# A macaron SwiGLU block on one core: the first products' deferred work in single small pieces, and the next norm's R11 and R22 made behind P2 and P5

## The chip, the core and the metric

The kernel runs on one core of a Trainium2 chip. A core has engines that run their own instruction streams side by side: TensorE (PE, matmuls; PEld is its loading of the stationary operand), VectorE (DVE), ScalarE (ACT), GpSimd (POOL, unused here) and SyncE (SP), which issues the DMA transfers. They meet through semaphores. Each engine runs its instructions in the order in which they stand in its stream. The metric is the device time of one execution in microseconds (us); the kernel before takes 2170.7 us (median of three runs, 2169.77 to 2173.17).

## The reference

One layer on an input x of 1024 tokens x 1024 channels, float32:

```python
def rmsnorm(x, g):
    xf = x.astype(jnp.float32)
    y = xf * lax.rsqrt(jnp.mean(xf * xf, axis=-1, keepdims=True) + NORM_EPS)
    return (y * g.astype(jnp.float32)).astype(x.dtype)

def swiglu_ffn(x, w_in, w_out):
    gate, up = jnp.split(x @ w_in, 2, axis=-1)
    return (jax.nn.silu(gate) * up) @ w_out
...
        h = h + FFN_RES_WEIGHT * swiglu_ffn(rmsnorm(h, norm_ffn1[l]), ffn1_w_in[l], ffn1_w_out[l])
        u = rmsnorm(h, norm_mix[l])
        proj = u @ w_in[l]
...
        h = h + merged @ w_out[l]
        h = h + FFN_RES_WEIGHT * swiglu_ffn(rmsnorm(h, norm_ffn2[l]), ffn2_w_in[l], ffn2_w_out[l])
    return rmsnorm(h, norm_final)
```

The hidden width of a SwiGLU is 2816, so `w_in` is 1024 x 5632. Between the SwiGLUs lie a combined projection, a retention and a pooling branch, their gated merge and an output projection, which the change doesn't touch.

## The kernel before

*Products.* Every large product is done as a 2 x 2 block scheme that trades block products for block sums (seven products of half-size blocks in place of eight). A token-side operand is called R (R11, R12, R21, R22 are its blocks, T1 to T4 and others are their sums and differences); a weight-side combination is S1 to S4 (`a_S`, lines 437, 450 and 454, on DVE). To keep float32 accuracy on the matmul's reduced type, each operand is split in an upper part (ACT, line 158 or 162) and a lower part, the remainder (DVE, line 159 or 163); `mm3` then issues three matmuls, upper x upper (line 178), upper x lower (179), lower x upper (180). A matmul at line 180 thus waits for the lower part of its weights. `mv` is the pool of split token-side operands, 28 tiles; `wS`, `wL`, `ws`, `wx`, `wy` are split weights (combinations, plain blocks and quarter-size sums).

*Stages.* With the times of the profiled execution: the first SwiGLU's input products (names `a_`, to some 410 us); its output products `b` in the order P1 with P6, P2 with P7, P5 (549 to 579 us), P3 (to 609) and P4 (to 639); the projections (`t0`, `t1`, `p0` and so on) with the norm `n2` from 639 us; retention, pooling and merge; the second SwiGLU's input products (`c_`, 1535 to 1945); its output products `d` with the final norm, to the end.

*The input products (`ffn_in`).* A group is one block of 128 gate and 128 up channels in each half of the block scheme; 22 groups are taken in 11 pairs (k and k + 11). When a group's products are evacuated (line 721 and 723 are sums of PSUM banks), `end()` hangs up what remains: the gate is multiplied by the norm's per-token factor (lines 735 and 738), silu is taken on ACT, and up is multiplied by gate (line 741, one instruction of 1024 columns). After the second group of a pair `w1`, `w2` and `w3` form the output products' token-side operands from the two results (lines 752, 753, 757, 762) and store them in R, T, B and T4 in DRAM by DMAs on SP's queue, from which the output products load them. The lines 571 and 582 collect the shared small products in the bank x.

*What sets the order.* A `Flow` runs the steps: each step has a `prep` (loads and splits), called four steps (`LOOK`) ahead, and a `body` (matmuls). Work of no hurry is put into a queue, `flow.add(...)`; after each body `flow.rate` pieces are taken from its head, and `flow.until` takes more where a result is needed at once. After that a scheduler of the tile framework orders the instructions of each engine by priority (the order of the program, with `soon()` ahead) and by its own estimate of what is ready. So a piece taken later is also placed later in DVE's stream, with what is written behind it put ahead. In FFN1's input products the rate is 1 for the first 40 steps and 2 then; in the second SwiGLU it is 1 for 14 steps and 2 then. A pair has 2 x 2 + 3 = 7 pieces.

*Output products and the next norm.* P1 to P7 are accumulated by `onto` and `done` into the sums `bacc`, whose last part is queued. The quarters of the result are final in the order of the products: the block (0,0) after P2, (1,1) after P5, (0,1) after P3 and (1,0) after P4. The next norm `n2` takes its operands from them: `r11`, `r22` (with `p22`, the split), `t1`, `t2`, `t3`, `r21`, `t4_`, four pieces each, and its statistics (`stats`: the sum of squares `n2sum`, the inverse root `n2v`, `n2r`, then its spread over the partitions by the diagonals `n20dg`, `n21dg` and the matmuls `n20b`, `n21b`, and the copies `n2rb`). `end(0)` queues six of these behind P3, `end(1)` the rest behind P4. P5's operands are called `bp5m`, P4's `bp4m`; they come from the same pool `mv` as the norm's.

Of the kernel before, what the change touches and what calls it, by code (L numbers as in the profile page):

```python
# [13 lines left out]
AF = mybir.ActivationFunctionType  # L14
ALU = mybir.AluOpType
ADD, SUB, MUL = ALU.add, ALU.subtract, ALU.mult
# [74 lines left out]
def block_kernel(ctx: ExitStack, tc, x, x_tok, vecs, f1_in, f1_out, w_in, w_v, pool_w, w_ret, w_pool, w_o,  # L91
# [3 lines left out]
    tt = nc.vector.tensor_tensor  # L95
    stt = nc.vector.scalar_tensor_tensor
    act = nc.scalar.activation
# [48 lines left out]
    def half(t, j):  # L146
        return t[:, j * H : (j + 1) * H]
# [553 lines left out]
    def ffn_in(nx, w, ops, name, start=None):  # L701

        R, T, B, T4 = ops
        hid = {}

        def group(g):
            gate_up = {}

            def dest(which):
                tile, j = which  # L710
                if tile not in gate_up:
                    gate_up[tile] = (tl if start and g == 0 else t4)(f"{name}{'gu'[tile]}{g}")
                return half(gate_up[tile], j)

            later = []

            def evac(which, in0, in1):
                tile, j = which
                dst, rms = dest(which), nx.rb
                if in1 is not None:  # L720
                    tt(dst, in0, in1, ADD)
                elif not tile and rms is not None:
                    tt(dst, in0, half(rms, j), MUL)
                    return
                else:
                    copy(dst, in0)
                if not tile:
                    later.append(j)

            def end():  # L730
                gate, up = gate_up[0], gate_up[1]

                def scale():
                    if len(later) == 2:
                        tt(gate, gate, nx.rms(), MUL)
                    else:
                        for j in later:
                            tt(half(gate, j), half(gate, j), half(nx.rms(), j), MUL)
                    act(gate, gate, AF.Silu)

                flow.add(scale, lambda: tt(up, gate, up, MUL))
                hid[g] = up
                k = g % FH
                if g < FH:
                    return
                lo, hi, e = hid.pop(k), up, {}
                R11, R12, R21, R22 = half(lo, 0), half(lo, 1), half(hi, 0), half(hi, 1)

                def w1():

                    e["n"], e["m"] = gate, c2(f"{name}m{k}")
                    tt(half(e["n"], 0), R12, R11, SUB)
                    tt(half(e["n"], 1), R22, R12, SUB)
                    load(B[k], e["n"])

                def w2():
                    tt(R12, R22, half(e["n"], 0), SUB)
                    load(R[k], lo)
                    load(T[k], hi)

                def w3():
                    tt(e["m"], R21, R12, SUB)
                    load(T4[k], e["m"])
                    done.add(k)

                flow.add(w1, w2, w3)

            if start and g == 0:
                return plain_group(nx, start, f"{name}{g}_", evac, end)
            return lambda shared: strassen(nx, w[g, 0], w[g, 1], f"{name}{g}_", evac, end, shared=shared, dest=dest)  # L770

        done = ops_done.setdefault(name, set())
        order = [g for k in range(FH) for g in (k, k + FH)]
        if start:

            return chain(group(0), pairs_of_both(nx, (group(g) for g in order[1:]), BY_OPERAND, 3))
        return pairs_of_both(nx, (group(g) for g in order), BY_OPERAND, 2)
# [31 lines left out]
    def ffn_out(nx, ops, ready, w, res, name, sink, end, last=None):  # L809
# [121 lines left out]
        def done(mt, j, to=sink, scaled=False):  # L931
            q = quarter(mt, j)

            def end():
                if not scaled:
                    scale(q, q, j)
                tt(q, q, old.pop((mt, j)), ADD)
                if to:
                    to(mt, slice(j * H, (j + 1) * H), acc[mt])

            flow.add(end)
# [9 lines left out]
        def after2(i):  # L951
            with soon():
                scale(quarter(i, 0), bk["a", i], 0)
            done(i, 0, scaled=True)

        def after7(i):
            onto(i + 4, 1, "b", i, p1s[i])
# [9 lines left out]
        def after5(i):  # L967
            onto(i + 4, 1, "a", i)
            done(i + 4, 1)

        def after3(i):
            onto(i, 1, "a", i)
            done(i, 1)
            if i == 3:
                end(0)

        def after4(i):
            onto(i + 4, 0, "b", i)
            done(i + 4, 0)
            if i == 3:  # L980
                end(1)

        for k in range(FH):
            yield step("p1", p1, k, "a", True, after1)
# [91 lines left out]

    def ffn1():
        for n, step in enumerate(ffn_in(first, f1_in, ops1, "a", lead)):
            flow.rate = 1 if n < 40 else 2
            yield step  # L1080
        yield from ffn_out(first, ops1, ops_done["a"], f1_out, x, "b", mix.quarter, end1)

    mix = Next("n2", V_MIX, h1)

    def end_of(nx):
        def end(part):
            if part == 0:
                nx.work(nx.r11, nx.r22, nx.t2, nx.t1, nx.t3, nx.p22)
            else:
                nx.work(nx.r21, nx.t4_)  # L1090
                nx.stats()

        return end
# [232 lines left out]
    def projections():  # L1326
        for n, step in enumerate(pairs(mix, (project(*o) for o in order), range(7), 0)):
            if n == 28:
                flow.rate = 1
            yield step  # L1330
        yield from values()
        for o in light[10:]:
            g = project(*o)(())
            yield from (g[m] for m in BY_SUM)
        flow.rate = 2
# [242 lines left out]
    def retention():  # L1578
        filler = fillers()

        def fill(n=1):
            for _ in range(n):
                f = next(filler, None)
                if f is not None:
                    yield f

        yield units[0].operands, units[0].values
        for n, u in enumerate(units):
            after = units[n + 1] if n + 1 < len(units) else None

            def scores(u=u, n=n):
                if u.nh == 1:
                    u.follow(units[n - 1])
                u.scores()

            def rest(u=u, after=after):
                u.products()
                if after:
                    after.operands()
                u.outputs()  # L1600
                if u.nh == 1:
                    u.normalise()

            yield none, scores
            yield none, u.keys
            yield from fill()
            if after:
                yield after.loads, after.values
            yield none, rest

            late = u.nh == 0 and n
            if n < 3 or late:
                yield from fill()
            if late:
                yield none, units[n - 1].finish
        yield none, lambda: take(range(6))
        yield from fill(2)
        yield none, units[-1].finish
        yield none, lambda: take((6, 7))
        yield from fill(2 * KT)  # L1620
# [85 lines left out]
    def merge():  # L1706
        yield from two_by_two(two_groups(0) + two_groups(1), BY_OPERAND, handed(mg, lambda rest: flow.add(*rest)))
        yield from two_by_two((out_group(i) for i in range(4)), BY_OPERAND,
                              handed(ffn2, lambda rest: (flow.add(*rest[:4]), ffn2.stats(between=rest[4:]))))
# [4 lines left out]
    class Last(Norm):  # L1714
# [74 lines left out]
            return r0  # L1789

        def end(self, part):
            tokens = slice(H, S)
            at = {}

            def stats():
                r = inverse_root(token_sums(self.ssq, range(tokens.start // P, tokens.stop // P), "fin0"), D, "fin0")
                at["b"] = spread(r, "fin0")

            def scale(mt):
                t = self.tiles[mt][:, tokens]  # L1800
                stt(t, t, vec[:, V_FINAL + mt : V_FINAL + mt + 1], at["b"], MUL, MUL)
                load(out[mt, :, tokens], t)

            flow.add(stats, *(lambda mt=mt: scale(mt) for mt in range(KT)))
# [2 lines left out]

    def second():
        for n, step in enumerate(ffn_in(ffn2, f2_in, ops2, "c")):
            flow.rate = 1 if n < 14 else 2  # L1810
            yield step
    flow.run(chain(ffn1(), projections(), retention(), merge(), second(),
                   ffn_out(ffn2, ops2, ops_done.setdefault("c", set()), f2_out, h2, "d", fin.quarter, fin.end, fin)))
    flow.some(-1)
# [86 lines left out]
```

## Time and profile before

| | us |
|---|---|
| median of three runs | 2170.7 (2169.77 to 2173.17) |
| profiled execution | 2170.95, span 2169.2 |
| PE busy | 2144.7 (99%) |
| DVE busy | 1839.2 (85%) |
| ACT busy | 1093.4 (50%) |

The span is the time from the first to the last recorded instruction. A row of a timeline gives start and duration in us, the engine, the line of the kernel, the operation, out<-in by the program's names with their numbers left out, the shapes, and in brackets the idle time of the engine before it and what ended it. Matmuls of 512 columns are shown 0.39 us long and start some 0.22 to 0.23 us apart, as they overlap in the array; a start-to-start time above that is a loss. DVE's instructions overlap a little too: one of 512 columns lasts 0.68 us and the next starts 0.60 us after it.

### The profile page before, as it was taken

The numbers are of one execution on the slowest core, as the hardware profiler recorded it, in microseconds if no ns is written. First come the engines' busy times: TensorE is split into PE (matmuls) and PEld (weight loads), VectorE is DVE, ScalarE is ACT, GpSimd is POOL, SyncE is SP. The second block draws the span as 40 slices with busy tenths as digits, with TensorE's granted clock in tenths as the row PEclk, the third lists the DMA queues.
The fourth block names the chain that finished last, engine by engine and source line by source line (L and its number), as shares of the span: only waits on it lengthen the run. The fifth ranks groups of instructions, "written<-read, shape, count | busy, mean of one in ns | idle before, by whom it ended". The sixth has DMA issues, their size and how long they took to land.

```text
span 2169.2 us, 29623 instructions
## 1 busy us (share of the span) xinstructions
PE 2144.7 (99%) x10668; PEld 1811.1 (83%) x10668; DVE 1839.2 (85%) x3180; ACT 1093.4 (50%) x2053; POOL 0.2 (0%) x4
## 2 busy tenths in 40 slices
PE   9999999999998999999999999999999999999998
PEld 7888888888887888888888898887888888888887
DVE  8789788896889798899767877899998878889697
ACT  8544444454646444444426754446644444445454
POOL 0000000000000000000000000000000000000000
PEclk9999999999999999999999999999999999999999
DMA  7233223585533333333485567624132222358633
GB/s 259 85 117 117 91 98 114 168 283 186 174 92 117 117 124 110 107 117 109 155 271 191 165 219 257 222 98 156 68 119 101 107 95 101 117 170 281 194 122 126
DMA packets 120131, 320.91 MB, mean 148 GB/s; under 512 B 13232, under 2 KB 17456, under 8 KB 119984
## 3 DMA queue, kind: packets, MB, share of 16 engines
q1 hardware_dynamic: 119408, 317.98, 43.1%
q8 instruction: 83, 1.36, 0.3%
q10 hardware_dynamic: 576, 1.05, 0.1%
q14 instruction: 64, 0.52, 0.1%
HBM read 228.27 MB, written 90.70 MB: 147 GB/s over the span
## 4 chain that ended last, share of the span: by engine, by line
PE 88%; DVE 8%; DMA 2%; issue 1%; ACT 1%; SPq 0%; ACTq 0%; DVEq 0%
PE c_b L180 2%; PE a_b L180 2%; PE c_b L179 2%; PE a_b L178 2%; PE c_b L178 2%; PE a_b L179 2%; PE a_e L178 1%; PE a_e L180 1%; PE a_e L179 1%; PE bp6b L179 1%; PE bp6b L178 1%; PE bp6b L180 1%; PE a_a L179 1%; PE a_a L178 1%; PE a_a L180 1%
## 5 line engine op out<-in xcount | busy, mean ns | idle before, releaser
L180 PE MATMUL c_b<-n3T,c_wS 128*128 128x512 f32 x176 | 69.3, 394 | 2.4 <-DVE c_wS L159 2.3
L178 PE MATMUL c_b<-n3T,c_wS 128*128 128x512 f32 x176 | 68.3, 390 | 1.4 <-ACT c_wS L158 1.4
L179 PE MATMUL c_b<-n3T,c_wS 128*128 128x512 f32 x176 | 68.5, 389 | 0.0
L180 PE MATMUL a_b<-n1T,a_wS 128*128 128x512 f32 x168 | 65.9, 392 | 2.0 <-DVE a_wS L159 2.0
L178 PE MATMUL a_b<-n1T,a_wS 128*128 128x512 f32 x168 | 65.5, 390 | 1.4 <-ACT a_wS L158 1.4
L179 PE MATMUL a_b<-n1T,a_wS 128*128 128x512 f32 x168 | 65.4, 389 | 0.0
L179 PE MATMUL a_a<-n1R,a_wL 128*128 128x512 f32 x120 | 46.7, 389 | 0.0
L178 PE MATMUL a_a<-n1R,a_wL 128*128 128x512 f32 x120 | 46.7, 389 | 0.0
L180 PE MATMUL a_a<-n1R,a_wL 128*128 128x512 f32 x120 | 46.7, 389 | 0.0
L179 PE MATMUL c_a<-n3R,c_wL 128*128 128x512 f32 x112 | 43.7, 390 | 0.0
L178 PE MATMUL c_a<-n3R,c_wL 128*128 128x512 f32 x112 | 43.6, 389 | 0.0
L180 PE MATMUL c_a<-n3R,c_wL 128*128 128x512 f32 x112 | 43.6, 389 | 0.0
L180 PEld LDWEIGHTS c_b<-n3T,c_wS 128*128 128x128 f32 x176 | 33.0, 188 | 12.1 <-DVE c_wS L159 5.4
L180 PEld LDWEIGHTS a_b<-n1T,a_wS 128*128 128x128 f32 x168 | 31.5, 188 | 10.5 <-DVE a_wS L159 4.1
L178 PEld LDWEIGHTS c_b<-n3T,c_wS 128*128 128x128 f32 x176 | 33.0, 188 | 8.4 <-ACT c_wS L158 1.8
L179 PEld LDWEIGHTS c_b<-n3T,c_wS 128*128 128x128 f32 x176 | 33.0, 188 | 6.9
L178 PEld LDWEIGHTS a_b<-n1T,a_wS 128*128 128x128 f32 x168 | 31.5, 188 | 8.2 <-ACT a_wS L158 1.8
L179 PEld LDWEIGHTS a_b<-n1T,a_wS 128*128 128x128 f32 x168 | 31.5, 188 | 6.5
L158 ACT CAST a_wS<-a_S 128x512 fp32r<-128x512 f32 x45 | 27.1, 621 | 17.1 <-DVE a_S L437 9.6
L178 PE MATMUL c_e<-n3T,c_wS 128*128 128x512 f32 x88 | 34.4, 391 | 0.0
L179 PE MATMUL c_e<-n3T,c_wL 128*128 128x512 f32 x88 | 34.4, 391 | 0.0
L178 PE MATMUL c_e<-n3T,c_wL 128*128 128x512 f32 x88 | 34.3, 390 | 0.0
(3063 smaller groups left out, 8030.5 us busy)
## 6 DMA issues: line engine op xcount, KB each, us to landing
c_ra<-in_f_in SPq DMA_DIRECT2D x22, 512.0 KB, 3.5
c_rb<-in_f_in SPq DMA_DIRECT2D x22, 512.0 KB, 3.6
a_ra<-in_f_in SPq DMA_DIRECT2D x21, 512.0 KB, 3.5
a_rb<-in_f_in SPq DMA_DIRECT2D x21, 512.0 KB, 4.2
t<-au SPq DMA_DIRECT2D x11, 512.0 KB, 2.6
b<-ag SPq DMA_DIRECT2D x11, 512.0 KB, 2.6
r<-au SPq DMA_DIRECT2D x11, 512.0 KB, 3.0
br<-r SPq DMA_DIRECT2D x11, 512.0 KB, 6.4
```

What stands on the lines that cost most here:

```text
L158: copy(hi, src)
L178: mm(dst, w[0], m[0], start=start, stop=False, skip_group_check=True)
L179: mm(dst, w[0], m[1], start=False, stop=False, skip_group_check=True)
L180: mm(dst, w[1], m[0], start=False, stop=stop, skip_group_check=True)
```

## The change

It has three parts. (1) In `end()` of the input products the queue gets smaller pieces: the norm's factor, then silu, then the two halves of up x gate one by one (`times(0)`, `times(1)`); `w1` is split after its first subtraction (`w1b` has the second and the load of B). A pair has 2 x 4 + 4 = 12 pieces. (2) The rate is 1 in all steps of both SwiGLUs' input products, and 2 afterwards. (3) `end` is called behind P2, P5, P3 and P4 of the output products: R11 of the next norm is queued behind P2, R22 with its split behind P5, T2, T1 and T3 behind P3, R21 and T4 with the statistics behind P4. The final norm's `end` (class `Last`) acts behind P3 alone, as it did.

```diff
--- before.py
+++ after.py
@@ -736,9 +736,11 @@
                     else:
                         for j in later:
                             tt(half(gate, j), half(gate, j), half(nx.rms(), j), MUL)
-                    act(gate, gate, AF.Silu)
-
-                flow.add(scale, lambda: tt(up, gate, up, MUL))
+
+                def times(j):
+                    tt(half(up, j), half(gate, j), half(up, j), MUL)
+
+                flow.add(scale, lambda: act(gate, gate, AF.Silu), lambda: times(0), lambda: times(1))
                 hid[g] = up
                 k = g % FH
                 if g < FH:
@@ -750,6 +752,8 @@
 
                     e["n"], e["m"] = gate, c2(f"{name}m{k}")
                     tt(half(e["n"], 0), R12, R11, SUB)
+
+                def w1b():
                     tt(half(e["n"], 1), R22, R12, SUB)
                     load(B[k], e["n"])
 
@@ -763,7 +767,7 @@
                     load(T4[k], e["m"])
                     done.add(k)
 
-                flow.add(w1, w2, w3)
+                flow.add(w1, w1b, w2, w3)
 
             if start and g == 0:
                 return plain_group(nx, start, f"{name}{g}_", evac, end)
@@ -952,6 +956,8 @@
             with soon():
                 scale(quarter(i, 0), bk["a", i], 0)
             done(i, 0, scaled=True)
+            if i == 3:
+                end(2)
 
         def after7(i):
             onto(i + 4, 1, "b", i, p1s[i])
@@ -967,18 +973,20 @@
         def after5(i):
             onto(i + 4, 1, "a", i)
             done(i + 4, 1)
+            if i == 3:
+                end(5)
 
         def after3(i):
             onto(i, 1, "a", i)
             done(i, 1)
             if i == 3:
-                end(0)
+                end(3)
 
         def after4(i):
             onto(i + 4, 0, "b", i)
             done(i + 4, 0)
             if i == 3:
-                end(1)
+                end(4)
 
         for k in range(FH):
             yield step("p1", p1, k, "a", True, after1)
@@ -1076,18 +1084,17 @@
 
     def ffn1():
         for n, step in enumerate(ffn_in(first, f1_in, ops1, "a", lead)):
-            flow.rate = 1 if n < 40 else 2
+            flow.rate = 1
             yield step
+        flow.rate = 2
         yield from ffn_out(first, ops1, ops_done["a"], f1_out, x, "b", mix.quarter, end1)
 
     mix = Next("n2", V_MIX, h1)
 
     def end_of(nx):
         def end(part):
-            if part == 0:
-                nx.work(nx.r11, nx.r22, nx.t2, nx.t1, nx.t3, nx.p22)
-            else:
-                nx.work(nx.r21, nx.t4_)
+            nx.work(*{2: (nx.r11,), 5: (nx.r22, nx.p22), 3: (nx.t2, nx.t1, nx.t3), 4: (nx.r21, nx.t4_)}[part])
+            if part == 4:
                 nx.stats()
 
         return end
@@ -1789,6 +1796,8 @@
             return r0
 
         def end(self, part):
+            if part != 3:
+                return
             tokens = slice(H, S)
             at = {}
 
@@ -1807,8 +1816,9 @@
 
     def second():
         for n, step in enumerate(ffn_in(ffn2, f2_in, ops2, "c")):
-            flow.rate = 1 if n < 14 else 2
+            flow.rate = 1
             yield step
+        flow.rate = 2
     flow.run(chain(ffn1(), projections(), retention(), merge(), second(),
                    ffn_out(ffn2, ops2, ops_done.setdefault("c", set()), f2_out, h2, "d", fin.quarter, fin.end, fin)))
     flow.some(-1)
```

Line numbers below this part move by 4 from the first hunk's end, so that 741 stays and 752, 753, 757 and 762 become 754, 757, 761 and 766.

DVE in the first SwiGLU's input products, at the pair of which the profile shows the stretch from 358 to 368 us; `a10` and `a21` are the groups coming in, `9` and `20` (`au9`, `ag20`, `am9`) those whose deferred pieces are left. Before:

```order
L741 TENSOR_TENSOR au20_3652<-ag20_3479,au20_3652 128x1024
L450 TENSOR_TENSOR a10_rb_3680<-a10_ra_3679,a10_rb_3680 128x512
L752 TENSOR_TENSOR ag20_3479<-au9_3635 128x512
L753 TENSOR_TENSOR ag20_3479<-au20_3652,au9_3635 128x512
L159 TENSOR_TENSOR a10_wS3_3797<-a10_rb_3680,a10_wS3_3797 128x512
L571 TENSOR_TENSOR ag10_3824<-a10_x2_3822,ag21_3825 128x256
L757 TENSOR_TENSOR au9_3635<-au20_3652,ag20_3479 128x512
L721 TENSOR_TENSOR ag10_3824<-a10_a_3772,ag10_3824 128x512
L762 TENSOR_TENSOR am9_3787<-au20_3652,au9_3635 128x512
L437 TENSOR_TENSOR a10_S2_3817<-a10_S1_3794,a10_ra_3679 128x512
L582 TENSOR_TENSOR ag21_3825<-a10_x2_3822,ag21_3825 128x256
L437 TENSOR_TENSOR a21_S1_3846<-a21_rb_3701 128x512
```

After, the same place, about the weight `a10_wS2`:

```order
L450 TENSOR_TENSOR a21_rb_3719<-a21_ra_3718,a21_rb_3719 128x512
L437 TENSOR_TENSOR a21_S2_3875<-a21_S1_3854,a21_ra_3718 128x512
L571 TENSOR_TENSOR ag10_3831<-a10_x2_3829,ag21_3832 128x256
L159 TENSOR_TENSOR a10_wS2_3826<-a10_S2_3824,a10_wS2_3826 128x512
L721 TENSOR_TENSOR ag10_3831<-a10_a_3786,ag10_3831 128x512
L159 TENSOR_TENSOR a21_wS3_3857<-a21_rb_3719,a21_wS3_3857 128x512
L582 TENSOR_TENSOR ag21_3832<-a10_x2_3829,ag21_3832 128x256
L159 TENSOR_TENSOR a21_wS2_3877<-a21_S2_3875,a21_wS2_3877 128x512
L721 TENSOR_TENSOR ag21_3832<-a21_a_3808,ag21_3832 128x512
L741 TENSOR_TENSOR au20_3670<-ag20_3484,au20_3670 128x512
L454 TENSOR_TENSOR a10_S2_3824<-a10_ra_3697,a10_S2_3824 128x512
L159 TENSOR_TENSOR a10_wS1_3897<-a10_S1_3802,a10_wS1_3897 128x512
```

Before, au20's product, both subtractions of `w1`, `w2` and `w3` stand ahead of `a10_S2`; `a10_wS2` follows four rows behind. After, `a10_wS2` and `a21_wS3`, `a21_wS2` stand ahead of au20's first half, and the pieces of `w1` to `w3` come behind that.

TensorE at the start of the projections, at the spread of the norm's inverse root (`n20b`, `n21b`). Before:

```order
L178 MATMUL t1e_6149<-n2T41_6142,t1wL22_6246 128x512
L246 MATMUL n20b_6212<-n20dg0_6216,ones_r_91 128x512
L179 MATMUL t1e_6149<-n2T41_6142,t1wL22_6246 128x512
L246 MATMUL n20b_6212<-n20dg1_6222,ones_r_91 128x512
L180 MATMUL t1e_6149<-n2T41_6142,t1wL22_6246 128x512
L178 MATMUL t1e_6149<-n2T42_6168,t1wL22_6246 128x512
L179 MATMUL t1e_6149<-n2T42_6168,t1wL22_6246 128x512
```

After:

```order
L179 MATMUL t1a_6044<-n2R213_6086,t1wL12_6138 128x512
L180 MATMUL t1a_6044<-n2R213_6086,t1wL12_6138 128x512
L246 MATMUL n20b_6174<-n20dg0_6178,ones_r_91 128x512
L246 MATMUL n20b_6174<-n20dg1_6184,ones_r_91 128x512
L246 MATMUL n21b_6191<-n21dg0_6195,ones_r_91 128x512
L246 MATMUL n21b_6191<-n21dg1_6201,ones_r_91 128x512
L178 MATMUL t0e_6212<-n2T30_5882,t0wS3_6066 128x512
L179 MATMUL t0e_6212<-n2T30_5882,t0wS3_6066 128x512
```

Before, the spread stands among the last products of t1 (`t1wL22`); after, it stands behind t1a's product with R21 (`n2R213`), ahead of the runs t0e, t1e, t0b, t1b, t0e, t1e that had stood before it.

DVE at the end of P4 (`bp4`), where the first plain weights of the projections (`t0wL11`) are split. Before:

```order
L159 TENSOR_TENSOR bp4m10_5830<-bT410_5825,bp4m10_5830 128x512
L313 SCALAR_TENSOR_TENSOR bacc2_4339<-n2t12_5845,neg_67,bacc6_4343 128x512
L159 TENSOR_TENSOR bp4w10_5827<-bL2210_5823,bp4w10_5827 128x512
L318 TENSOR_TENSOR n2t13_5851<-bacc3_4340 128x512
L159 TENSOR_TENSOR n2T22_5848<-bacc2_4339,n2T22_5848 128x512
L313 SCALAR_TENSOR_TENSOR bacc3_4340<-n2t13_5851,neg_67,bacc7_4344 128x512
L159 TENSOR_TENSOR t0wL11_5861<-t0ra_5857,t0wL11_5861 128x512
L437 TENSOR_TENSOR t0S1_5907<-t0rb_5858 128x512
```

After:

```order
L159 TENSOR_TENSOR n2T31_5886<-bacc1_4360,n2T31_5886 128x512
L159 TENSOR_TENSOR bp4m10_5896<-bT410_5891,bp4m10_5896 128x512
L313 SCALAR_TENSOR_TENSOR bacc2_4361<-bacc2_4361,neg_67,bacc6_4365 128x512
L313 SCALAR_TENSOR_TENSOR bacc3_4362<-bacc3_4362,neg_67,bacc7_4366 128x512
L930 TENSOR_TENSOR bacc4_4363<-bp6b0_4191,bacc4_4363 128x512
L930 TENSOR_TENSOR bacc5_4364<-bp6b1_4192,bacc5_4364 128x512
L930 TENSOR_TENSOR bacc6_4365<-bp6b2_4193,bacc6_4365 128x512
L930 TENSOR_TENSOR bacc7_4366<-bp6b3_4194,bacc7_4366 128x512
L159 TENSOR_TENSOR n2T32_5912<-bacc2_4361,n2T32_5912 128x512
L159 TENSOR_TENSOR n2T33_5916<-bacc3_4362,n2T33_5916 128x512
L159 TENSOR_TENSOR t0wL11_5923<-t0ra_5919,t0wL11_5923 128x512
```

Before, `t0wL11` follows P4's last operand by six rows, ahead of P4's results; after, it stands behind the four sums of P4's results (`bacc4` to `bacc7` from the banks `bp6b0` to `bp6b3`) and two parts of T3 (`n2T3`).

## The prediction

> **What bounds the kernel now.** I read the page's busy line first, then the waits of TensorE, then the timelines at the longest of them and the busy time by stretch.
>
> The busy line of the page:
>
> ```profile
> span 2169.2 us, 29623 instructions
> PE 2144.7 (99%) x10668; PEld 1811.1 (83%) x10668; DVE 1839.2 (85%) x3180; ACT 1093.4 (50%) x2053; POOL 0.2 (0%) x4
> ```
>
> TensorE is idle for 2169.2 - 2144.7 = 24.5 us. The change removes no matmul, so it can gain only what TensorE waits, with the time it loses on starting up again. VectorE (DVE) has 330 us free over the span, but not evenly. TensorE's waits, by what it waited for (total us, times, longest):
>
> ```profile
> PE p0e L178 <- ACT p0wS L158: 5.7, 1, 5.7
> PE c_b L180 <- DVE c_wS L159: 2.3, 6, 0.5
> PE a_b L180 <- DVE a_wS L159: 2.0, 5, 0.5
> PE a_b L178 <- ACT a_wS L158: 1.4, 1, 1.4
> PE c_b L178 <- ACT c_wS L158: 1.4, 1, 1.4
> ...
> PE a_e L178 <- ACT a_wS L158: 0.7, 1, 0.7
> ...
> PE a_x L178 <- DVE ag L571: 0.4, 1, 0.4
> ```
>
> The six lines with `a_` or `c_` are the first products of the two SwiGLUs: 2.3 + 2.0 + 1.4 + 1.4 + 0.7 + 0.4 = 8.2 us in 15 waits. All but the last wait for a block combination of weights (`a_wS`), whose lower part DVE makes. The first line is the start of the projections, behind the first SwiGLU's last product. These two places are the ones that the change touches.
>
> What one short wait costs, on TensorE's timeline near 367 us (start, duration):
>
> ```profile
> 366.16 0.39 PE L178 MATMUL a_b<-n1T,a_wS 128*128 128x512 f32 x1
> 366.39 0.39 PE L179 MATMUL a_b<-n1T,a_wS 128*128 128x512 f32 x1
> 367.14 0.50 PE L180 MATMUL a_b<-n1T,a_wS 128*128 128x512 f32 x1 [0.36 <-DVE a_wS L159]
> 367.48 0.39 PE L178 MATMUL a_b<-n1T,a_wS 128*128 128x512 f32 x1
> 367.71 0.40 PE L179 MATMUL a_b<-n1T,a_wS 128*128 128x512 f32 x1
> ```
>
> Undisturbed matmuls start 0.23 us apart. Here the steps are 0.75 and 0.34, an excess of 0.52 + 0.11 = 0.63 us for 0.36 idle: a wait costs its idle time and about 0.27 more.
>
> What DVE did before it, from its timeline:
>
> ```profile
> 358.59 1.21 DVE L741 TENSOR_TENSOR au<-ag,au 128x1024 f32<-128x1024 f32 x1
> 359.73 0.68 DVE L450 TENSOR_TENSOR a_rb<-a_ra,a_rb 128x512 f32<-128x512 f32 x1
> 360.33 0.68 DVE L752 TENSOR_TENSOR ag<-au 128x512 f32<-128x512 f32 x1
> 360.93 0.68 DVE L753 TENSOR_TENSOR ag<-au,au 128x512 f32<-128x512 f32 x1
> ...
> 362.47 0.68 DVE L757 TENSOR_TENSOR au<-au,ag 128x512 f32<-128x512 f32 x1
> ...
> 363.67 0.68 DVE L762 TENSOR_TENSOR am<-au,au 128x512 f32<-128x512 f32 x1
> 364.27 0.68 DVE L437 TENSOR_TENSOR a_S<-a_S,a_ra 128x512 f32<-128x512 f32 x1
> ...
> 366.41 0.68 DVE L159 TENSOR_TENSOR a_wS<-a_S,a_wS 128x512 fp32r<-128x512 f32 x1
> ```
>
> Five deferred pieces (one L741 of 1.14 us by its start to the next, four of 0.60) stand ahead of the weights. They serve nobody soon: their results are stored for the last products. Busy time by stretch (length, then busy us of PE, PEld, DVE, ACT, POOL, the granted clock, the DMA share, GB/s):
>
> ```profile
> 329.00:367.00 38.00, 37.44 (x205) 32.13 (x204) 32.08 (x55) 18.02 (x33) 0.00 (x0) 1.00 0.30 105
> 1773.00:1810.00 37.00, 36.98 (x204) 32.18 (x204) 31.08 (x54) 17.18 (x32) 0.00 (x0) 1.00 0.32 108
> 610.00:640.00 30.00, 30.00 (x134) 24.86 (x133) 30.00 (x49) 14.47 (x25) 0.00 (x0) 1.00 0.46 144
> 640.00:668.00 28.00, 28.00 (x133) 23.30 (x132) 27.04 (x45) 17.01 (x31) 0.00 (x0) 1.00 0.16 57
> 668.00:683.00 15.00, 15.00 (x67) 12.00 (x65) 13.23 (x33) 10.44 (x22) 0.00 (x0) 1.00 0.31 105
> 683.00:689.00 6.00, 0.29 (x2) 0.11 (x1) 6.00 (x14) 4.80 (x8) 0.00 (x0) 0.69 0.43 175
> ```
>
> In a pair of groups (first two rows) DVE has some 5.9 us free; what is late there is late by its place in DVE's queue. Between 610 and 689 it is all but full (30.00 + 27.04 + 13.23 + 6.00 = 76.3 of 79 us), and behind it TensorE stops at 683: there the amount of DVE's work is the bound.
>
> **The change, part by part.**
>
> *Deferred pieces, one a step.* Each au*ag becomes two halves: 2 x 0.60 against 1.14, so 0.06 us more of DVE, 44 times, 2.6 us, hidden by the 5.9 us free in each pair. Each pair's L752 and L753 become two pieces. In the changed order, ahead of the weight `a_wS2` for the place at 367 us stand only the first group's halves; the other's product, L752, L753, L757 and L762 (1.2 + 4 x 0.60 = 3.6 us) have gone behind the weights, and three others (1.8 us) have come forward. So that weight comes at least 1.8 us sooner, and 0.36 was missing: the wait goes. The 1.4 us waits (one in each SwiGLU) are on the same tile, made some 15 us sooner in the new order. If all 15 waits go, 8.2 + 15 x 0.27 = 12.3 us are gained; if nothing of it happened, 0.
>
> What is late next: the pieces now stand among the next products' evacuations, where the x bank is freed (L571). The a_x row above prices one such wait at 0.4 + 0.27 = 0.7 us. The blocks of the norm's R21 and R22 have their operands made a little later too, once for each in either SwiGLU; by the same row 4 x 0.7 = 2.8 us at most if all four wait, and I take two, 1.4. The stores of `au` and `ag` on SP's queue follow the pieces by a step or two and are read a product later. Net: 12.3 - 1.4 = 10.9 us gained (between 0 and 12.3).
>
> *rate 2 afterwards* is what the last products had already: nothing. *Behind P2 and P5:* R11, R22 and their combination are made from P2's end on, in place of P3's. Their eight split tiles come out of the pool that also holds P5's and P4's operands, so these are made later. P5's come some 5 us ahead of need, by the DVE rows between at 0.60 us each: I cost that at nothing; if that cover is gone, one wait is 0.36 + 0.27. For P4 the new order has six of its eleven `bp4m` made ahead, where it had ten; five fall into P4, whose DVE time is full (30.00 of 30.00 in the third row). Four lower parts of R22 leave it. The sum of DVE's work up to the projections is unchanged, the order within isn't:
>
> ```profile
> 629.36 0.69 DVE L159 TENSOR_TENSOR t0wL<-t0ra,t0wL 128x512 fp32r<-128x512 f32 x1
> ...
> 637.55 2.54 DVE L926 TENSOR_TENSOR bacc<-bp6b,bacc 128x512 f32<-128x512 f32 x4
> 640.01 0.68 DVE L159 TENSOR_TENSOR n2T<-bacc,n2T 128x512 fp32r<-128x512 f32 x1
> ...
> 672.46 0.15 DVE L214 TENSOR_SCALAR n2v<-n2sum 128x8 f32<-128x8 f32 x1
> ...
> 677.30 0.28 DVE L243 TENSOR_SCALAR n20dg<-cst,n20r 128x128 fp32r<-128x128 f32 x1
> ```
>
> ```profile
> L180 PE MATMUL t0a<-n2R,t0wL x8: 389/389/389, 639.7 to 663.5; 128*128 128x512 f32 x8
> ```
>
> ```profile
> 682.79 0.39 PE L180 MATMUL p0a<-n2R,p0wL 128*128 128x512 f32 x1
> 688.89 0.79 PE L178 MATMUL p0e<-n2T,p0wS 128*128 128x512 f32 x1 [5.71 <-ACT p0wS L158]
> 689.48 0.63 PE L179 MATMUL p0e<-n2T,p0wS 128*128 128x512 f32 x1
> ...
> 691.61 0.63 PE L178 MATMUL p0e<-n2T,p0wS 128*128 128x512 f32 x1
> 692.04 0.46 PE L179 MATMUL p0e<-n2T,p0wS 128*128 128x512 f32 x1
> ...
> 693.26 0.39 PE L178 MATMUL p0b<-n2T,p0wS 128*128 128x512 f32 x1
> ```
>
> Before, from the end of p0a (682.79 + 0.23 = 683.02) to p0b (693.26) pass 10.24 us, and twelve matmuls need 12 x 0.227 = 2.72: 7.5 us are lost, 5.7 of them idle and the rest matmuls at about 0.43 us apart behind it (the last rows). In the new order TensorE waits earlier, by my reading at four places:
> - P4's late operands (`bp4m10` is now behind five other DVE rows): about 0.9 us.
> - `t0wL11`, at 629.36 before, is now behind the four L926 (which cannot start before their products end, 637.55) and two n2T: 637.55 + 2.46 + 3 x 0.60 = 641.8, where t0a's L180 wanted it at 639.7. About 2.2 us.
> - t0a and t1a of R21 now come before t0e; from t0wL11 to their `t0wL12` are 34 DVE rows at 0.60 to 0.66, so some 21 us to 663; TensorE has six products (6 x 2.72) and n2sum till then and is there at 659.5. About 3.5 us.
> - The norm's spread, n20b and n21b, stands ahead of five runs of products now. From n2v to the last n20dg DVE took 677.30 + 0.28 - 672.46 = 5.1 us, and n2v comes about 3.5 us behind t0wL12, so n20dg is there 8 us after it; TensorE has 24 matmuls (5.4 us) meanwhile. With n21dg about 3.7 us.
>
> Sum 10.3, with 4 x 0.27 of starting up 11.4; and a clock term. The granted clock is 1.00 in every stretch above but the last (0.69), with the 5.71 us wait, and the matmuls behind it start 0.43 us apart for 3 us; the excess above idle and start is 7.5 - 5.7 - 0.3 = 1.5 us. None of the new waits is as long, so I take a third of it, 0.5: 11.9 in all. p0e itself then doesn't wait: its weight, by the same count of DVE rows, is there at 689, and TensorE arrives at 694. So 11.9 lost in place of 7.5: 4.4 us worse (bounds: 7.5 better, were all waits gone; 8 worse, were each a half longer).
>
> [...]
>
> *Sum:* -10.9 + 4.4 = -6.5 us. The profiled run took 2170.95 us, 0.25 above the median of the three, 2170.7. So 2164.5 by the run, and I say **2164.5 us**.
>
> **The rivals.** Within 0.2% means 4.3 us either way, about what a measurement can tell here.
> - *The projections are no worse* (0.20). DVE is all but full from 610 to 689 in both orders, and TensorE has 5.7 us of slack there; if the earlier waits together stay under that, p0e still sets the stage. Then -10.9 + 0 = 2160, and down to 2153 if p0e's wait is gone as well. Against it: my four waits add up to twice the slack.
> - *The waits only move* (0.22; the other side). DVE serves in order: seven pieces become twelve, one in nearly every step, so each lower part of a weight has one ahead of it. If each of the 15 waits turns up elsewhere (a_x's bank, R21, R22), the first part is worth 0, and with +4.4 the time is 2175.4. It decides from 10.9 us kept. For it: the pieces do stand ahead of some L159 in the new order. Against it: 5.9 us are free in each pair.
> - *Cold twice* (0.12): both waits of 3.5 and 3.7 us lower the clock as the one of 5.7 did, 2 x 1.5 in place of 0.5, which gives 2167. For it: they are nearer to 5.7 than to 1.4. Against: no row shows such a wait.
> - *It doesn't do it* (0.06): the new order of weights is as late as the old, no wait goes or comes: 2170.7.
>
> **How the numbers follow.** My forecast has 0.40, with 2162 to 2168 of its own. Faster by over 0.2% is under 2166.4: 0.30 of the forecast's 0.40, the first rival's 0.20, 0.05 of the third: 0.55. Slower is over 2175: 0.16 of the second and 0.04 of the forecast's own (the transition at its upper bound and more): 0.20. Within lie 0.06 of the forecast, 0.06 of the second, 0.07 of the third and the fourth's 0.06: 0.25. The range, 2157 to 2176, leaves out half of the first rival's lower reach and what of the second lies above, about 0.15.
>
> **What would show it.** In the profile of the changed kernel: the lines a_b and c_b <- a_wS, c_wS gone from TensorE's waits, and a_x or c_x lines not over 1.5 us together; p0e <- p0wS gone, and in its place t0a <- t0wL and n20b or n21b <- n2's diagonals, some 10 us together; the half clock near 672, or none. The prediction is wrong if waits of the a_ and c_ lines stay above 5 us, if P5's bp5m stops TensorE, or if the waits from 610 to 700 add up to less than 6 or more than 15 us.

## The result and the profile after

The changed kernel takes 2169.0 us (median of 20 runs, 2166.4 to 2171.6), the kernel before 2171.2 (20 runs beside them). The ratio is 0.9990, 95% interval 0.9983 to 0.9997: about 2 us faster, a difference that the interval just tells from nothing. The forecast was 2164.5, by a sum of -6.5 us, with the range from 2157 to 2176. Here and below, medians and ratios leave out single slow executions of several thousand us (one in E2, one in E10, two of the kernel before). The profiled run took 2169.06 us, its span 2167.2.

TensorE's waits in the changed kernel (total us, times, longest):

```profile
PE t0b L178 <- ACT t0v L479: 3.2, 1, 3.2
PE t0a L180 <- DVE t0wL L159: 2.5, 1, 2.5
PE n20b L246 <- ACT n20dg L245: 2.2, 1, 2.2
PE n21b L246 <- ACT n21dg L245: 1.6, 1, 1.6
...
PE c_x L178 <- DVE cg L571: 0.7, 1, 0.7
...
PE a_x L178 <- DVE ag L571: 0.5, 1, 0.5
```

All waits for `a_wS` and `c_wS` are gone: 8.2 us of idle time in the first products have become 1.2, at the x bank. So is the wait of p0e for p0wS (5.7). In its place stand four waits at the projections' start, 9.5 us together.

At the first products, the place quoted for the kernel before (there L180 of a_b waited at 367 us) is some 4 us earlier now, on TensorE and on DVE:

```profile
362.38 0.39 PE L178 MATMUL a_b<-n1T,a_wS 128*128 128x512 f32 x1
362.60 0.39 PE L179 MATMUL a_b<-n1T,a_wS 128*128 128x512 f32 x1
362.83 0.39 PE L180 MATMUL a_b<-n1T,a_wS 128*128 128x512 f32 x1
```

```profile
358.69 0.68 DVE L159 TENSOR_TENSOR a_wS<-a_S,a_wS 128x512 fp32r<-128x512 f32 x1
...
362.03 0.68 DVE L741 TENSOR_TENSOR au<-ag,au 128x512 f32<-128x512 f32 x1
```

The lower part of the weight is begun at 358.69 and wanted at 362.83; the second group's first half of up x gate comes behind it, at 362.03.

The busy time by stretch at the end of P4 and the start of the projections (length, busy us of PE, PEld, DVE, ACT, POOL, the granted clock, the DMA share, GB/s):

```profile
607.00:637.00 30.00, 27.50 (x121) 21.88 (x119) 30.00 (x50) 15.90 (x28) 0.00 (x0) 1.00 0.46 140
637.00:665.00 28.00, 24.82 (x105) 20.23 (x106) 26.85 (x48) 16.39 (x28) 0.00 (x0) 0.88 0.17 61
665.00:680.00 15.00, 11.26 (x36) 8.48 (x35) 5.26 (x16) 6.09 (x16) 0.00 (x0) 0.77 0.17 63
```

TensorE has holes in all three, and the granted clock is below 1 in two, where before it was so behind p0e alone. DVE, which had been busy 13.2 of 15 us from 668 to 683, has only 5.3 of 15 from 665 to 680: it runs dry there.

The sum, by the excess of matmuls' start-to-start times over the undisturbed ones in the two profiled runs (us lost; steps with under 0.04 us of excess are left out):

| place | before | after | difference |
|---|---|---|---|
| first products of the first SwiGLU | 8.2 | 3.1 | -5.1 |
| first products of the second SwiGLU | 7.3 | 3.2 | -4.1 |
| end of P4 to p0b | 7.9 | 16.6 | +8.7 |
| all other places | 11.6 | 10.5 | -1.0 |

That is -1.5, against -2.0 us in the spans. The gain was made and nearly all of it was given back at one place.

### The profile page after: what moved, and what is told of

It reads as the page before. It is cut to its first block, busy times and chain, and to the rows that moved or that the text cites. A ratio compares the mean times of both kernels' runs of the same rounds, so it can differ in the third digit from the quotient of the medians.

```text
span 2167.2 us, 29645 instructions
## 1 busy us (share of the span) xinstructions
PE 2145.4 (99%) x10668; PEld 1815.0 (84%) x10668; DVE 1837.3 (85%) x3223; ACT 1091.1 (50%) x2053; POOL 0.2 (0%) x4
## 3 DMA queue, kind: packets, MB, share of 16 engines
q10 hardware_dynamic: 576, 1.05, 0.1%
## 4 chain that ended last, share of the span: by engine, by line
PE 91%; DVE 6%; ACT 1%; DMA 1%; issue 1%; SPq 0%; ACTq 0%; DVEq 0%
PE c_b L178 2%; PE c_b L180 2%; PE c_b L179 2%; PE a_b L178 2%; PE a_b L180 2%; PE a_b L179 2%; PE c_e L178 2%; PE c_e L179 2%; PE c_e L180 2%; PE a_e L178 2%; PE a_e L179 2%; PE a_e L180 2%; PE c_a L179 1%; PE a_a L178 1%; PE c_a L178 1%; PE c_a L180 1%
## 5 line engine op out<-in xcount | busy, mean ns | idle before, releaser
L180 PE MATMUL c_b<-n3T,c_wS 128*128 128x512 f32 x176 | 68.5, 389 | 0.0
L180 PE MATMUL a_b<-n1T,a_wS 128*128 128x512 f32 x168 | 65.4, 389 | 0.0
L180 PE MATMUL a_a<-n1R,a_wL 128*128 128x512 f32 x120 | 46.7, 389 | 0.0
L180 PE MATMUL c_a<-n3R,c_wL 128*128 128x512 f32 x112 | 43.6, 389 | 0.0
L180 PEld LDWEIGHTS c_b<-n3T,c_wS 128*128 128x128 f32 x176 | 33.0, 188 | 6.9
L159 DVE TENSOR_TENSOR a_wS<-a_S,a_wS 128x512 fp32r<-128x512 f32 x45 | 30.6, 682 | 9.1 <-ACT a_wS L158 9.0
L180 PEld LDWEIGHTS a_b<-n1T,a_wS 128*128 128x128 f32 x168 | 31.5, 188 | 6.6
L159 DVE TENSOR_TENSOR c_wS<-c_S,c_wS 128x512 fp32r<-128x512 f32 x46 | 31.3, 681 | 3.6 <-ACT c_wS L158 3.6
L178 PE MATMUL c_e<-n3T,c_wL 128*128 128x512 f32 x88 | 34.4, 391 | 0.0
```

The source lines that it names most:

```text
L159: tt(lo, src, hi.bitcast(F32), SUB)
L178: mm(dst, w[0], m[0], start=start, stop=False, skip_group_check=True)
L180: mm(dst, w[1], m[0], start=False, stop=stop, skip_group_check=True)
```

## The experiments

The ratio is always to the kernel before, run on the same chip beside it; 0.001 is 2.2 us. "Lost" is the excess as in the table above.

### The two parts apart

E1 has the pieces and the rate, with the next norm's work behind P3 and P4 as before:

```diff
-            nx.work(*{2: (nx.r11,), 5: (nx.r22, nx.p22), 3: (nx.t2, nx.t1, nx.t3), 4: (nx.r21, nx.t4_)}[part])
-            if part == 4:
+            if part == 0:
+                nx.work(nx.r11, nx.r22, nx.t2, nx.t1, nx.t3, nx.p22)
+            else:
+                nx.work(nx.r21, nx.t4_)
                 nx.stats()
```

> Parts 1 and 2 of the change (pieces and rate), with the next norm's work behind P3 and P4 as before. Theory A (two separate parts): the 9.3 us that the changed kernel saved in the two SwiGLUs' first products stay (start-to-start losses 15.5 us before, 6.3 after), and the start of the projections loses the 7.9 us that it lost before, with the wait of p0e for p0wS at 5.7 us: about 2162 us, ratio 0.9957. Theory B (the pieces themselves shift the projections' start): the projections lose some 16 us here too: about 2170 us.

Measured: 2159.6 us, ratio 0.9952 (0.9939 to 0.9964), 10.1 us faster. The first products lost 4.6 us, the projections' start 8.8, and its wait is the old one:

```profile
PE p0e L178 <- ACT p0wS L158: 5.7, 1, 5.7
```

E2 is the opposite: the four calls of `end` alone, with seven pieces and the old rates.

```diff
-                flow.add(scale, lambda: act(gate, gate, AF.Silu), lambda: times(0), lambda: times(1))
+                flow.add(scale, lambda: tt(up, gate, up, MUL))
...
-            flow.rate = 1
+            flow.rate = 1 if n < 40 else 2
```

> Part 3 of the change alone: R11 behind P2, R22 behind P5, T2, T1 and T3 behind P3, R21 and T4 behind P4. Theory A: the first products wait as before (8.2 us of idle in 15 waits) and the projections' start loses 16.2 in place of 7.9 us: about 2179.5 us, ratio 1.0038. Theory B: no slower than 2173 us.

Measured: 2179.0 us (median of four), ratio 1.0041 (1.0027 to 1.0054), 9 us slower. Both runs answer theory A. E2's waits are those of the kernel before in the first products and those of the changed kernel at the projections' start:

```profile
PE t0b L178 <- ACT t0v L479: 3.2, 1, 3.2
PE t0a L180 <- DVE t0wL L159: 2.5, 1, 2.5
PE c_b L180 <- DVE c_wS L159: 2.3, 6, 0.5
PE n20b L246 <- ACT n20dg L245: 2.2, 1, 2.2
PE a_b L180 <- DVE a_wS L159: 2.0, 5, 0.5
PE n21b L246 <- ACT n21dg L245: 1.6, 1, 1.6
```

By ratios, -0.0048 and +0.0041 add up to -0.0007, and the whole change has -0.0010: the parts hardly touch each other.

### Size of a piece, or their number a step

E3 has twelve pieces at the old rates, E4 seven pieces at rate 1.

```diff
-            flow.rate = 1
+            flow.rate = 1 if n < 40 else 2
```

> Part 1 alone: twelve smaller pieces a pair, at the old rates (2 a step after step 40 and step 14). Theory A, the size of a piece is what held the weights up: nearly the whole gain, 2163 to 2165 us. Theory B, how many are taken a step is: with two pieces a step most waits for the weights stay, gain 0 to 4 us, 2167 to 2171 us.

```diff
-                flow.add(scale, lambda: act(gate, gate, AF.Silu), lambda: times(0), lambda: times(1))
+                flow.add(scale, lambda: tt(up, gate, up, MUL))
...
-                flow.add(w1, w1b, w2, w3)
+                flow.add(w1, w2, w3)
```

> Part 2 alone: seven pieces a pair as before, one a step throughout. Theory A (size): the product of 1024 columns and both subtractions of w1 still stand ahead of the weights, gain 0 to 4 us, 2167 to 2171 us. Theory B (number a step): the weights come ahead, 2162 to 2165 us.

Measured: E3 2162.0 us, ratio 0.9962 (0.9949 to 0.9974); E4 2160.6 us, ratio 0.9959 (0.9945 to 0.9972). Each edit's own theory came out (the times lie 1 us below its range), and the theory against it was wrong: either edit brings most of the gain alone. In both, the last subtractions of `w1` to `w3` stand behind the weight of the place quoted above, which is begun 4.2 us ahead of its use (at 359.66 for 363.84 in E3, at 358.88 for 363.05 in E4). The first products lost 7.1 us in E3, 5.2 in E4, 4.6 with both. With the rate at 1, the smaller pieces add nothing that these runs can tell (intervals of 0.9939 to 0.9964 and 0.9945 to 0.9972).

### Which of the moved operands

E5 moves R11 alone, E6 R22 with its split alone; both have the new pieces and rate.

```diff
-            nx.work(*{2: (nx.r11,), 5: (nx.r22, nx.p22), 3: (nx.t2, nx.t1, nx.t3), 4: (nx.r21, nx.t4_)}[part])
+            nx.work(*{2: (nx.r11,), 5: (), 3: (nx.r22, nx.t2, nx.t1, nx.t3, nx.p22), 4: (nx.r21, nx.t4_)}[part])
```

> The change with R11 alone moved (behind P2); R22 with its split is made behind P3 again, as before the change. Eight of P4's eleven operands are made ahead of P3's results (ten without the moves, six with both). Theory A, the moved operands' tiles are what costs, each four alike: half of the 10.2 us that the moves cost alone, so about 2165 us. Theory B, it is the order at the projections' start (the norm's spread ahead of t0e) and not the number: that order is a different one here, with the spread among t0b's products, and the time is within 2 us of the first products alone, 2160 to 2162 us.

```diff
-            nx.work(*{2: (nx.r11,), 5: (nx.r22, nx.p22), 3: (nx.t2, nx.t1, nx.t3), 4: (nx.r21, nx.t4_)}[part])
+            nx.work(*{2: (), 5: (nx.r22, nx.p22), 3: (nx.r11, nx.t2, nx.t1, nx.t3), 4: (nx.r21, nx.t4_)}[part])
```

> The change with R22 and its split moved alone (behind P5); R11 is made behind P3 again. Eight of P4's eleven operands come ahead of P3's results, as with R11 alone. Theory A (each four operands moved cost alike): 2164 to 2167 us, as with R11 alone (2166.3). Theory B (the place of the norm's spread ahead of t0e, which this kernel shares with the full change and R11 alone does not): near the full change, 2167 to 2170 us, with waits of n20b and n21b of 3 us or more.

Measured: E5 2166.3 us, ratio 0.9977 (0.9968 to 0.9987); E6 2166.2 us, ratio 0.9982 (0.9973 to 0.9991). They are alike in time, as theory A had it (E6's waits at the spread are those of its theory B). Against E1 (0.9952) R11 costs 0.0025, R22 0.0030, both 0.0038; with intervals of 0.001 to either side, whether each costs half of the whole or more isn't told. TensorE's waits in E5, then in E6:

```profile
PE t0b L178 <- ACT t0v L479: 5.7, 1, 5.7
PE p0e L178 <- ACT p0wS L158: 1.5, 1, 1.5
```

```profile
PE t0b L178 <- ACT t0v L479: 4.4, 1, 4.4
PE n20b L246 <- ACT n20dg L245: 2.2, 1, 2.2
PE n21b L246 <- ACT n21dg L245: 1.6, 1, 1.6
```

The wait of t0a for t0wL (2.5 us) needs both moves; the wait for t0v comes with either.

### The wait that the forecast didn't have

In the changed kernel t0b waits for `t0v`, the copy of a PSUM bank on ACT. ACT's timeline there:

```profile
646.82 0.63 ACT L264 ACTIVATE n2q<-bacc 128x512 f32<-128x512 f32 x1 [1.16 <-DVE bacc L941]
...
649.23 0.63 ACT L264 ACTIVATE n2q<-bacc 128x512 f32<-128x512 f32 x1 [1.16 <-DVE bacc L941]
649.76 0.57 ACT L479 COPY t0v<-t0b 128x512 f32<-128x512 f32 x1
```

TensorE's last product ahead of it starts at 646.82. The copy stands behind squares of the norm, which wait for DVE's sums. E7 makes the two copies on VectorE, E10 leaves them on ScalarE but takes their tiles from another pool:

```diff
-                copy(u("v"), t["b"])
+                (nc.vector.tensor_copy if name in ("t0", "t1") else copy)(u("v"), t["b"])
```

> The changed kernel with the copies of t0v and t1v (PSUM bank to SBUF, line 479) on VectorE in place of ScalarE, where they stand behind squares that wait for VectorE. Theory A, the wait of t0b is one of a chain: it goes with its half clock (3.2 + 2.65 us), but t0a then waits some 3.5 us for t0wL of L12, so that 2 to 3 us are gained, 2166 to 2167 us. Theory B, it stands alone: 6 us gained, 2163 us.

```diff
-            t[n] = c2(f"{name}{n}")
+            t[n] = half(tl(f"{name}{n}"), 0) if name in ("t0", "t1") and n == "v" else c2(f"{name}{n}")
```

> The changed kernel with t0v and t1v in the pool tl in place of c2 (c2 also holds the squares n2q and the sums t1 of the norm). Theory A: what held the copy t0v, on ScalarE and on VectorE alike, was its tile, which came free with n2ssq<-n2q; in ScalarE's order it now stands two squares sooner, t0b's wait (3.2 us) and its half clock go, and part of it is given back at t0a of L12, whose t0wL is there 3 us later: gain 1 to 4 us, 2165 to 2168 us. Theory B: the copy wasn't held by its tile, and the wait of t0b stays at 3 us or more.

Measured: E7 2168.2 us, ratio 0.9988 (0.9979 to 0.9997): nothing gained over the change (0.9990), and both theories missed. The copy came nearly as late on DVE, from 648.93 to 649.61, and t0b waited 3.4 us, to 649.76. The profile puts this wait down to `n2R` on ACT (L162), which ended at 649.62; which of the two held t0b isn't shown. E10: 2167.9 us, ratio 0.9991 (0.9982 to 1.0000), nothing gained either, but here the wait of t0b is gone. Its waits:

```profile
PE t0a L180 <- DVE t0wL L159: 2.5, 1, 2.5
PE n20b L246 <- ACT n20dg L245: 2.2, 1, 2.2
PE n21b L246 <- ACT n21dg L245: 1.6, 1, 1.6
...
PE t0a L178 <- ACT t0wL L158: 1.1, 1, 1.1
PE t1a L178 <- ACT t1wL L158: 0.8, 1, 0.8
```

So theory A's mechanism held in E10: with a tile from another pool than `c2`, which the norm's squares fill, the copy stands two squares sooner on ACT, at 646.73, and t0b doesn't wait. But its size didn't hold: nearly all of the time came back, 1.9 us at t0a and t1a of L12, and in matmuls at the half clock: from 658.86 on, behind those two waits (1.05 and 0.83 us), they start 0.43 us apart, and the granted clock was 0.89 from 637 to 668 us and again from 668 to 700 us. The projections' start lost 15.8 us in E10 and 16.3 in E7, against 16.6.

### The place of the norm's spread

E9 is the changed kernel with empty pieces in the deferred queue, so that the spread is queued some steps later:

```diff
-                nx.stats()
+                nx.stats(between=[lambda: None] * 6)
```

> The changed kernel with six empty pieces between the norm's inverse root and its spread, by which n20b and n21b come behind t0e, t1e, t0a and t1a in TensorE's order. Theory A: the waits of n20b and n21b (2.2 + 1.6 us) with the half clock behind them (2.65 us) go, 2162 to 2164 us. Theory B, VectorE or ScalarE is the bound there: the time turns up at another wait before p0b, 2167 to 2169 us.

Measured: 2161.5 us (2156.9 to 2163.2), ratio 0.9952 (0.9939 to 0.9965): 7.5 us less than the changed kernel, as theory A had it. The projections' start lost 10.0 us; what is left is two waits, and behind the second row's, from 638.43 to 641.41, matmuls at half clock, 0.43 us apart:

```profile
PE t0b L178 <- ACT t0v L479: 3.0, 1, 3.0
PE t0a L180 <- DVE t0wL L159: 2.5, 1, 2.5
```

With this one edit the moves of R11 and R22 cost nothing against E1 (0.9952 too). They don't gain anything either: E11 below, with a later spread and without the moves, has 0.9940, and the two intervals overlap.

### Versions beyond both kernels

E8 is E1 without the return to rate 2 behind the first SwiGLU's first products:

```diff
             yield step
-        flow.rate = 2
         yield from ffn_out(first, ops1, ops_done["a"], f1_out, x, "b", mix.quarter, end1)
```

> Parts 1 and 2 without the moves, and the rate left at 1 in the first SwiGLU's last products and the mixer too (it is set to 2 only after the second SwiGLU's first products). The weight p0wS then stands ahead of the norm's statistics in VectorE's order. Theory A: the wait of p0e for p0wS (5.7 us) and the half clock behind it go, 2152 to 2155 us. Theory B, VectorE's work before the projections is the bound whatever its order: the wait turns up at another product, 2158 to 2162 us.

Measured: 2168.5 us, ratio 0.9987 (0.9978 to 0.9997), 8 us slower than E1: both theories missed. The weight p0wS was early and p0e didn't wait, but the norm itself came late, and TensorE waited for its operands and its spread instead:

```profile
PE n20b L246 <- ACT n20dg L245: 3.5, 1, 3.5
PE t0a L179 <- DVE n2R L163: 2.9, 1, 2.9
PE t0a L178 <- ACT n2R L162: 2.7, 1, 2.7
```

E11 delays the spread alone, on E1:

```diff
-                nx.stats()
+                nx.stats(between=[lambda: None] * 8)
```

> Parts 1 and 2 without the moves (2160 us), with eight empty pieces between the norm's inverse root and its spread. VectorE's products with the spread (ten of 0.60 us ahead of p0wS before) come behind p0wS, which stands 23 rows sooner in its order. Theory A: p0e's wait (5.7 us) and its half clock (2 to 3 us) go: 2151 to 2154 us. Theory B, the amount of VectorE's work is the bound whatever its order: another wait of 3 us or more before p1's products, 2156 to 2160 us.

Measured: 2156.3 us, ratio 0.9940 (0.9927 to 0.9954). p0e's wait is gone, the granted clock is 1.00 from 605 to 700 us, and 3.4 us are lost there in place of 8.8. By time it falls at the lower edge of theory B, by its waits between the two: n21b 1.6 and n20b 1.1 us are new. E12 is E11 with two tiles for the root's split halves:

```diff
-        r2 = sb.tile([P, 2, 8], F32R, tag="r2", bufs=1, name=f"{name}r2")
+        r2 = sb.tile([P, 2, 8], F32R, tag="r2", bufs=2, name=f"{name}r2")
```

> As the first products alone with the spread later (2156.3 us), with two tiles in place of one for the inverse root's split halves (r2), so that the second half's need not wait for the first half's diagonals. Theory A: n21b's wait (1.6 us) and the 0.3 us of starting up go: 2154 to 2155 us. Theory B: ScalarE's and VectorE's rows ahead of the diagonals are as long, and the wait only moves: 2156 us.

Measured: 2152.9 us, ratio 0.9923 (0.9910 to 0.9935), 17 us less than the kernel before, the fastest here; lost at the projections' start: 1.5 us. It gained 1 to 2 us more than theory A allowed; the trace shows 2 us of it at n20b and n21b (now one wait of 0.7), and the rest was not followed up.

## Why the prediction was right, and where it was not

The direction and the two places were right, the size was not: the gain is a third of the one forecast, and the time lies in the range because the range was wide.

- *The waits for weights in the first products go; 10.9 us net.* Right. E1 alone gained 10.1; the excess fell by 9.2 in the changed kernel. What is left idle is at the bank x (0.5, where 0.4 was before, and 0.7), about the size of the two waits that I took of four, but those were at the norm's R21 and R22 blocks, where no such wait shows: the size is right by luck.
- *The weight comes at least 1.8 us sooner.* Right in kind, low in size: it was begun 4.1 us ahead of its use, where it had been late.
- *P5 does not wait.* Right, no such row. *P4's operands 0.9 us:* too much; the excess of P4's matmuls was about 0.3 us.
- *t0a for t0wL11, 2.2 us:* right, 2.5. *n20b and n21b, 3.7 us:* right, 2.2 + 1.6. *p0e does not wait:* right.
- *t0a for t0wL12, 3.5 us:* wrong. t0b waited for t0v instead, 3.2 us, and TensorE reached t0a so late that its weights were there. I had followed DVE's order and not that of ACT, nor the pool `c2` in which the norm's squares and t0v meet. In E10, without that wait, t0a and t1a of L12 wait 1.9 us, for the upper parts of their weights on ACT (L158) and not for the lower ones that I had counted on DVE. That the idle times add up to nearly the 10.3 us of the sum is partly luck: the wait at t0b stands in for this one and for P4's.
- *The clock term, 0.5 us:* this is the step that failed in size. The four waits were 9.5 us idle against 10.3 in the sum, but two stretches ran at half clock behind them:

```profile
650.38 0.80 PE L178 MATMUL t0b<-n2T,t0wS 128*128 128x512 f32 x1 [3.18 <-ACT t0v L479]
650.98 0.63 PE L179 MATMUL t0b<-n2T,t0wS 128*128 128x512 f32 x1
...
655.67 0.54 PE L178 MATMUL t1b<-n2T,t1wS 128*128 128x512 f32 x1
...
670.53 0.80 PE L246 MATMUL n21b<-n21dg,ones_r 128*128 128x512 f32 x1 [1.57 <-ACT n21dg L245]
...
676.59 0.40 PE L178 MATMUL t1e<-n2T,t1wS 128*128 128x512 f32 x1
```

From 650.98 to 655.67 eleven matmuls take 4.69 us where 11 x 0.227 = 2.5 would do, and with the steps at the edges 2.7 us are lost; from 670.53 to 676.59 likewise 2.9. That is 5.6 us where the sum had 0.5 for the clock and 0.27 for each of two starts. The 1.5 us of which I took a third was itself a low price: in the kernel before, more than half of the stretch at half clock passed while TensorE still waited (3.57 of 6.83 us, last section). The excess at the place was forecast as 11.9 and measured as 16.6, 8.7 us worse than before: beyond my upper bound of 8, which is what the idle times alone give when each is made a half longer. Put in for it, the forecast's sum becomes -10.9 + 8.7 = -2.2 us. This is the result, with two smaller errors that nearly cancel: the first products gave 9.2, and all other places 1.0.

Of the rivals, the third (*cold twice*) is what happened, though the first wait with half clock behind it was at t0b and not at t0a of L12; it was priced at 1.5 us a stretch from the kernel before, and with some 2.8 for each it would have given 2169 or 2170. *The waits only move* was wrong in the first products (E1). *The projections are no worse* was wrong by E2. I gave 0.55 to more than 0.2% faster and 0.25 to what came.

## What to carry to other kernels

Deferred work of no hurry belongs behind the operands that the next product needs, in an in-order engine's queue: one piece a step in place of two gave 9 us of 2170 with no arithmetic changed. Making an operand earlier is not free, since it shifts what is queued behind it on every engine (E5 and E6 each cost 5 us and more against E1), and a small chain (an inverse root and its spread) that stands ahead of independent matmuls in TensorE's order stops them all (2.2 us at n20b and 1.6 us at n21b in the changed kernel). Read the order of every engine in that chain, its pools included, before a wait is priced, and price a wait of TensorE both with and without a stretch at half clock behind it: of the waits here one of 3.2 us (the change) and one of 2.5 (E9) had such a stretch behind them, while one of 2.5 (the change) and one of 3.4 (E7) were followed by full speed.

## What was not expected of the hardware

The half clock did not follow the length of the single wait. It came behind waits of 5.7 us (kernel before, E1) and 3.2 (the change), behind 1.6 that followed a wait of 2.2 with two matmuls between (the change), and behind 1.05 and 0.83 in E10. A wait of 2.5 us at t0a was followed by none in the change, and in E9 by one from 638.4 on, 1.4 us behind the wait. In E7 a wait of 3.4 us was followed by full speed, the matmuls from 650.07 to 651.92 0.23 us apart:

```profile
649.76 0.47 PE L178 MATMUL t0b<-n2T,t0wS 128*128 128x512 f32 x1 [3.40 <-ACT n2R L162]
650.07 0.40 PE L179 MATMUL t0b<-n2T,t0wS 128*128 128x512 f32 x1
650.30 0.40 PE L180 MATMUL t0b<-n2T,t0wS 128*128 128x512 f32 x1
```

The granted clock shows when it fell. In the profiles of the two kernels it is 1.00 from 10 to 2160 us but for three stretches at 0.50 of 6.83 us each: from 685.32 in the kernel before, from 649.16 and from 669.64 in the changed one. Each began while TensorE waited. By stretch (length, busy us of PE, PEld, DVE, ACT, POOL, the granted clock, the DMA share, GB/s), the changed kernel from the start of t0b's wait to the end of the half clock:

```profile
647.21:649.16 1.95, 0.00 (x0) 0.00 (x0) 1.95 (x5) 0.85 (x2) 0.00 (x0) 1.00 0.35 134
649.16:650.38 1.22, 0.00 (x0) 0.00 (x0) 1.22 (x3) 1.15 (x3) 0.00 (x0) 0.50 0.28 111
650.38:655.99 5.61, 5.61 (x13) 4.45 (x14) 5.61 (x10) 3.38 (x7) 0.00 (x0) 0.50 0.06 24
```

The clock fell 1.95 us into this wait, 0.68 us into the wait of n21b (668.96 to 670.53) and 2.14 us into that of p0e in the kernel before, while the 2.5 us at t0a of the changed kernel brought no fall. What sets the moment of the fall, and the length of the stretch, these runs don't show.

Nor did the same instructions always get the same clock: the four executions of E2 took 2176.8, 2177.9, 2180.0 and 2181.1 us at mean granted clocks of 0.997, 0.996, 0.995 and 0.994.

The moment of the fall also shows why the kernel before gave too low a price. Its stretches at the wait of p0e:

```profile
683.18:685.32 2.14, 0.00 (x0) 0.00 (x0) 2.14 (x4) 1.37 (x3) 0.00 (x0) 1.00 0.36 147
685.32:688.89 3.57, 0.00 (x1) 0.00 (x1) 3.57 (x9) 3.14 (x6) 0.00 (x0) 0.50 0.50 205
688.89:692.14 3.25, 3.25 (x8) 2.45 (x9) 3.25 (x8) 3.25 (x7) 0.00 (x0) 0.50 0.41 166
```

Half clock was granted from 685.32 on, and TensorE waited until 688.89: only seven matmuls were slow. In E1, with the same wait (5.67 us), twelve were slow, from 682.59 to 687.86.
